# The v stage of a hybrid decoder layer: tile norms, transposes and sums placed ahead of the former tile's products, norm_g broadcast by a matmul, four store buffers

## The chip, the cores and the metric

The kernel runs on one core of a Trainium2 chip. A core has five engines that each work through a queue of their own in order: TensorE (PE) multiplies matrices and transposes, VectorE (DVE) and GpSimd (POOL) do elementwise work, ScalarE (ACT) does functions, copies and casts, and SyncE (SP) issues most of the DMA transfers. They meet only through semaphores. The metric is the device time of one execution in microseconds (us); lower is better.

## The reference

The layer norms its input `x` (1024 tokens by 1024 channels), projects it with one wide matrix `w_in`, runs a gated short convolution and a dilated attention beside each other, merges both by two gates, projects again and adds the residue. Cut to what matters here:

```
def rms_norm(x, g):
    xf = x.astype(jnp.float32)
    y = xf * lax.rsqrt(jnp.mean(xf * xf, axis=-1, keepdims=True) + EPS)
    return (y * g.astype(jnp.float32)).astype(x.dtype)
...
    u = rms_norm(h, norm_g[layer])
...
    proj = jnp.einsum("bsd,dc->bsc", h, w_in)
    xc, bg, cg, zc, q, k, v, za, g_conv, g_attn = jnp.split(proj, splits, axis=-1)
```

The v stage computes the columns `v` of `proj`, a product of 1024x1024 by 1024x1024, and on the way leaves the normed, transposed input in on-chip memory for all later stages.

## The kernel before

Every matrix product is done exactly in float32 by splitting both operands into a high and a low part (float32r) and adding three products: high by high, high by low, low by high. `split` (L77) makes the parts: ACT casts the source to the high part, then DVE, or POOL where it is named, subtracts to get the low part.

The v stage (L125 to L283) is the first of the kernel. The tokens come in eight tiles of 128. `normed(t)` takes one: ACT squares and sums it, `rstd_of` makes the scale in four small DVE operations and one ACT square root, DVE scales the two halves by the scale and by `gb` (norm_g times -0.5, on all 128 partitions), and PE transposes each half by four 128x128 transposes into banks 6 and 7 of PSUM. `into` splits a transposed half into the tables `b11`, `b21` (tiles 0 to 3) and `b22` (tiles 4 to 7).

The product uses seven block products in place of eight, after Strassen and Winograd. The sums of the input blocks, `t1` to `t4`, are made by `sums(j)` from tile 4+j and the tables of tile j: six DVE operations of 128x512 (L194 to L202), each result split again, with the low half on POOL. The sums of weight blocks are made on DVE from `piece`s of 512 KB (two of eight row blocks, all columns of one half), and split by `operand`. `prod` issues six PE products (two row blocks, three each) of 128x512, so one tile of one block product is two calls, 12 products. `added` and `emit` add what was kept aside, split the result and store it to `v_dram`.

The order is: for each of the tiles 0 to 3 in turn, `normed`, `into`, its b11 products, its b21 products, `added` (L231 to L241). Then the weight sums, `sums(0)` to `sums(3)`, and the block products t1, t2, b22, t3 and t4, each for all four tiles, by halves of the weight rows (`product`, L250). A scheduler reorders instructions within each engine's queue by its own times and by when buffers come free; so what stands in the code is not quite what stands in a queue. Buffers that matter: three slots for x tiles (`xt`), four for raw weights (`raw`), four for split weights (`v_hi`, `v_lo`), two for split results before their store (`v2`), eight PSUM banks.

After the v stage, `sec` (L293) computes all other column blocks in the same way, with weights in place of tokens as the split operand (`a_hi`, `a_lo`).

Of the kernel before, what the change touches and what calls it, by code (L numbers as in the profile page):

```python
# [11 lines left out]
F32 = mybir.dt.float32  # L12
F32R = mybir.dt.float32r
AF = mybir.ActivationFunctionType
OP = mybir.AluOpType
# [3 lines left out]
P = 128  # L19
S = 1024  # L20
D = 1024
# [2 lines left out]
LAST = (4, 6, 0, 2)  # L24
ACTP = 5
ACTL = 3
WARM = 22
HD = 64
NP = NH // 2
NB = S // P  # L30
# [10 lines left out]
def layer(ctx, tc, x, norm_g, w_blk, w_v, b_merge, conv_w, w_conv, w_attn, w_o, final_g, tab, sel_in, selb_in, out):  # L41
    nc = tc.nc
    ctx.enter_context(nc.allow_low_precision("float32 operands are split exactly into float32r pairs"))

    const = ctx.enter_context(tc.tile_pool(name="const", bufs=1, reuse_waits="tile"))
# [3 lines left out]
    ps = ctx.enter_context(tc.tile_pool(name="ps", bufs=1, space=PSUM))  # L49
# [22 lines left out]
    def bank(first=0, n=8):  # L72

        i = turn[first, n] = (turn.get((first, n), -1) + 1) % n
        return ps.tile([P, 512], F32, tag=f"bank{first + i}", name="bank")
# [42 lines left out]
    H = NK // 2  # L118
# [6 lines left out]
    with tc.tile_pool(name="p0", bufs=2, reuse_waits="tile") as p0:  # L125
        gb = p0.tile([P, D], F32, name="gb", bufs=1)
        xt = {}

        def load_x(i):
            xt[i] = p0.tile([P, D], F32, name="xt", bufs=3)  # L130
            nc.sync.dma_start(xt[i], x[i * P:(i + 1) * P, :])

        def piece(c, d, kh):

            raw = wr.tile([P, 2, 512], F32, tag="raw", name="raw")
            k = 4 * d + 2 * kh
            nc.sync.dma_start(raw, w_v[c, :, k:k + 2, :])
            return raw

        def operand(raw, eng=None):  # L140
            hi = p0.tile([P, 2, 512], F32R, name="v_hi", bufs=4)
            lo = p0.tile([P, 2, 512], F32R, name="v_lo", bufs=4)
            split(hi, lo, raw, eng)
            return hi, lo


        warm = bank(6, 2)
        for _ in range(WARM):
            nc.tensor.transpose(warm[:, :P], ident, ident)
        load_x(0)  # L150
        nc.sync.dma_start(gb, norm_g.to_broadcast([P, D]))
        nc.vector.tensor_scalar(gb, gb, -0.5, None, op0=OP.mult)
        raws = [piece(0, 0, 0), piece(0, 0, 1)]
        load_x(1)
        raws += [piece(0, 1, 0), piece(0, 1, 1)]
        load_x(2)
        a1 = [operand(r, nc.gpsimd if i else nc.vector) for i, r in enumerate(raws)]

        def normed(t):

            if t + 3 < NB:
                load_x(t + 3)
            sq = p0.tile([P, D], mybir.dt.bfloat16, tag="vc", name="sq")
            ss = small.tile([P, 1], F32, name="ss")
            nc.scalar.activation(sq, xt[t], AF.Square, accum_out=ss)
            rs = small.tile([P, 1], F32, name="rs")
            rstd_of(ss, rs)
            xs = xt[t]
            for g in range(2):
                gs = slice(g * 512, g * 512 + 512)  # L170
                nc.vector.scalar_tensor_tensor(xs[:, gs], xt[t][:, gs], rs, gb[:, gs], op0=OP.mult, op1=OP.mult)
                pt = bank(6, 2).rearrange("p (k q) -> p k q", k=4)
                for k in range(4):
                    nc.tensor.transpose(pt[:, k, :], xs[:, (4 * g + k) * P:(4 * g + k + 1) * P], ident)
                yield pt

        def into(n, j, src, eng=None):
            tt = slice(j * P, (j + 1) * P)
            split(ub[n][0][:, :, tt], ub[n][1][:, :, tt], src, eng)

        def of(n, j):
            return [f(y[:, :, j * P:(j + 1) * P]) for y in ub[n]]

        def sums(j):

            c12 = p0.tile([P, H, P], F32, name="c12", bufs=1)
            c22 = p0.tile([P, H, P], F32, name="c22", bufs=1)
            for n, pt in enumerate(normed(H + j)):
                nc.scalar.copy(c22 if n else c12, pt)
                if n:  # L190
                    into("b22", j, pt)
            t1, t2, t4 = (p0.tile([P, H, P], F32, name="ts", bufs=3) for _ in range(3))
            b11, b21 = of("b11", j), of("b21", j)
            nc.vector.tensor_sub(t1, c12, b11[0])  # L194
            nc.vector.tensor_sub(t1, t1, b11[1])
            into("t1", j, t1, nc.gpsimd)
            nc.vector.tensor_sub(t2, c22, t1)
            into("t2", j, t2, nc.gpsimd)
            nc.vector.tensor_sub(c12, c22, c12)
            into("t3", j, c12, nc.gpsimd)  # L200
            nc.vector.tensor_sub(t4, b21[0], t2)
            nc.vector.tensor_add(t4, t4, b21[1])  # L202
            into("t4", j, t4, nc.gpsimd)

        def prod(pt, n, j, kh, op, first=False):

            tt = slice(j * P, (j + 1) * P)
            bhi, blo = ub[n]
            hi, lo = op
            for i in range(2):  # L210
                k = 2 * kh + i
                more = dict(skip_group_check=not first)
                nc.tensor.matmul(pt, bhi[:, k, tt], hi[:, i, :], start=first and k == 0, stop=False, **more)  # L213
                nc.tensor.matmul(pt, bhi[:, k, tt], lo[:, i, :], start=False, stop=False, **more)  # L214
                nc.tensor.matmul(pt, blo[:, k, tt], hi[:, i, :], start=False, stop=k == H - 1, **more)

        def emit(c, t, v):
            v2 = p0.tile([P, 8, 2, HD], F32R, name="v2")
            split(v2[:, :, 0, :], v2[:, :, 1, :], v.rearrange("p (h d) -> p h d", h=8))
            nc.sync.dma_start(  # L220
                v_dram[4 * c:4 * c + 4, :, t * 256:(t + 1) * 256].rearrange("n p e -> p n e"),
                f(v2).rearrange("p (n a) s d -> p n (a s d)", n=4))

        def added(c, t, pt, v):
            vc = p0.tile([P, 512], F32, name="vc")
            nc.vector.tensor_add(vc, pt, v)
            emit(c, t, vc)

        chain = [ps.tile([P, 512], F32, tag=f"bank{j}", name="bank") for j in range(H)]
        x1 = []  # L230
        for j in range(H):  # L231
            for n, pt in zip(("b11", "b21"), normed(j)):
                into(n, j, pt)
            for kh in range(2):
                prod(chain[j], "b11", j, kh, a1[kh], first=True)
            x1.append(p0.tile([P, 512], F32, name="keep1", bufs=4))
            nc.scalar.copy(x1[j], chain[j])
            pt = bank(4, 2)
            for kh in range(2):
                prod(pt, "b21", j, kh, a1[2 + kh], first=True)  # L240
            added(0, j, pt, x1[j])  # L241
        sum_ = []
        for kh in range(2):
            r1, r2 = piece(1, 0, kh), piece(1, 1, kh)
            nc.vector.tensor_add(r1, r1, r2)
            sum_.append(r1)
        for j in range(H):
            sums(j)

        def product(n, pts, ops, first=False):  # L250
            for kh in range(2):
                for j in range(H):
                    prod(pts[j], n, j, kh, ops[kh], first)

        side = [ps.tile([P, 512], F32, tag=f"bank{4 + j}", name="bank") for j in range(H)]
        product("t1", side, [operand(r) for r in sum_], first=True)
        x5 = []
        for j in range(H):
            x5.append(p0.tile([P, 512], F32, name="keep1", bufs=4))
            nc.scalar.copy(x5[j], side[j])  # L260
        for kh in range(2):
            nc.vector.tensor_sub(sum_[kh], sum_[kh], piece(0, 0, kh))
        product("t2", chain, [operand(r) for r in sum_])
        u2 = []
        for j in range(H):
            u2.append(p0.tile([P, 512], F32, name="keep2", bufs=4))
            nc.scalar.copy(u2[j], chain[j])
        for kh in range(2):
            nc.vector.tensor_sub(sum_[kh], piece(0, 1, kh), sum_[kh])
        product("b22", side, [operand(r) for r in sum_])  # L270
        for j in range(H):
            added(0, H + j, side[j], u2[j])
        ops = []
        for kh in range(2):
            r1, r2 = piece(0, 0, kh), piece(1, 0, kh)
            nc.vector.tensor_sub(r1, r1, r2)
            ops.append(operand(r1))
        product("t3", chain, ops)
        for j in range(H):
            added(1, H + j, chain[j], x5[j])  # L280
        product("t4", chain, [operand(piece(1, 1, kh)) for kh in range(2)])
        for j in range(H):
            emit(1, j, chain[j])  # L283
# [497 lines left out]
```

## Time and profile before

| | us |
|---|---|
| median of 3 runs | 1374.81 |
| lowest, highest | 1372.64, 1378.58 |
| the profiled execution | 1380.34 |
| its span | 1378.5 |

| engine | busy us | share of span | instructions |
|---|---|---|---|
| PE | 1304.9 | 95% | 6228 |
| DVE | 843.0 | 61% | 1576 |
| ACT | 645.8 | 47% | 1265 |
| POOL | 257.8 | 19% | 187 |

The page has the whole span in 40 slices of about 34 us, one digit each for the tenths that an engine is busy. PE has 6, 5, 7 and 9 in the first four, and 8 or 9 from then to the last but one. The v stage lies in the first four and a half. The row of the granted clock has 8, 8, 7 and 9 tenths there and 9 or more after it. The chain of work that ended last is 85% PE over the whole span, 6% DMA, 3% each DVE, ACT and time without a cause in the profile ("issue").

A row of a timeline is start, duration, engine, line, operation, written tile, read tiles, shape and count; in brackets stands how long the engine was idle ahead of it and what released it. A PE row's duration contains the fill and drain of the array, so products follow one another in less than it: their pace is read from start to start.

### The profile page before, as it was taken

Reading aid. Unit: us, or ns where it says so; the run is one execution under the profiler, and the core shown is the slowest. Engines: PE = TensorE matmul, PEld = TensorE weight load, DVE = VectorE, ACT = ScalarE, POOL = GpSimd, SP = SyncE. Lnnn points to the kernel's source line nnn. Section 1 sums busy time; section 2 is a strip of 40 time slices with the busy share of each in tenths; the row PEclk is TensorE's granted clock in tenths of the full one; section 3 lists DMA queues with packets and bytes.
Section 4 is the critical chain, followed back from the end, with each engine's and each line's share of the span. In section 5 each row is a group of like instructions: output and inputs, shape, how many; then the busy total and the mean of one; then the engine's idle time right before and its main releaser. Section 6 shows DMA issues by size and latency. Waiting matters only on the chain.

```text
span 1378.5 us, 17657 instructions
## 1 busy us (share of the span) xinstructions
PE 1304.9 (95%) x6228; PEld 1080.1 (78%) x6228; DVE 843.0 (61%) x1576; ACT 645.8 (47%) x1265; POOL 257.8 (19%) x187
## 2 busy tenths in 40 slices
PE   6579899999999999999999998889999999999997
PEld 5358688888888888887888886778888888788886
DVE  3596566655767677676655443657667667554325
ACT  3444344444443434343444455767677768322211
POOL 2051000000010101011000000543444446254000
PEclk8879999999999999999999999999999999999999
DMA  7315444541222313136233324994566475655302
GB/s 259 120 49 198 155 167 168 171 165 62 77 92 62 123 62 107 49 113 197 101 110 112 115 84 114 312 261 135 152 169 161 134 194 188 219 168 186 150 31 92
DMA packets 87072, 192.38 MB, mean 140 GB/s; under 512 B 8456, under 2 KB 33292, under 8 KB 86856
## 3 DMA queue, kind: packets, MB, share of 16 engines
q1 hardware_dynamic: 84184, 182.32, 42.1%
q0 software_dynamic: 2800, 8.94, 1.9%
q8 instruction: 49, 0.80, 0.2%
q14 instruction: 39, 0.32, 0.1%
HBM read 132.91 MB, written 58.31 MB: 139 GB/s over the span
## 4 chain that ended last, share of the span: by engine, by line
PE 85%; DMA 6%; issue 3%; ACT 3%; DVE 3%; POOL 0%; SPq 0%; DVEq 0%; ACTq 0%
PE bank L314 16%; PE bank L315 16%; PE bank L316 16%; PE bank L96 4%; PE bank L98 4%; PE bank L97 4%; PE bank L548 3%; PE bank L559 2%; PE bank L560 2%; PE bank L719 2%; PE bank L717 2%; PE bank L718 2%; PE bank L213 2%; DMA kl<-qk_dram 2%; PE bank L214 2%
## 5 line engine op out<-in xcount | busy, mean ns | idle before, releaser
L314 PE MATMUL bank<-t_hi,a_hi 128*128 128x512 f32 x576 | 225.2, 391 | 2.7 <-DVE sec_o L325 2.3
L315 PE MATMUL bank<-t_lo,a_hi 128*128 128x512 f32 x576 | 224.8, 390 | 0.0
L316 PE MATMUL bank<-t_hi,a_lo 128*128 128x512 f32 x576 | 224.8, 390 | 0.0
L78 ACT CAST a_hi<-s 128x512 fp32r<-128x512 f32 x144 | 89.6, 622 | 191.4 <-PE bank L315 175.2
L314 PE MATMUL bank<-b_hi,a_hi 128*128 128x512 f32 x432 | 169.5, 392 | 4.7 <-ACT a_hi L78 4.7
L315 PE MATMUL bank<-b_lo,a_hi 128*128 128x512 f32 x432 | 168.8, 391 | 0.0
L316 PE MATMUL bank<-b_hi,a_lo 128*128 128x512 f32 x432 | 168.5, 390 | 0.0
L79 DVE TENSOR_TENSOR a_lo<-s,a_hi 128x512 fp32r<-128x512 f32 x144 | 102.1, 709 | 100.1 <-ACT a_hi L78 100.0
L78 ACT CAST a_hi<-raw 128x512 fp32r<-128x512 f32 x108 | 67.1, 621 | 149.3 <-PE bank L315 126.0
L314 PEld LDWEIGHTS bank<-t_hi,a_hi 128*128 128x128 f32 x576 | 108.5, 188 | 25.9 <-DVE sec_o L325 3.0
L315 PEld LDWEIGHTS bank<-t_lo,a_hi 128*128 128x128 f32 x576 | 108.6, 189 | 22.6
L316 PEld LDWEIGHTS bank<-t_hi,a_lo 128*128 128x128 f32 x576 | 108.4, 188 | 22.6
L440 ACT ACTIVATE pr<-pr,nm 128x640 f32<-128x640 f32 (+7 forms) x128 | 99.9, 782 | 24.7 <-DVE nm L435 24.3
L435 DVE CUSTOM_DVE_ANT_0 pr<-bank,bias 128x512 f32<-128x512 f32 (+3 forms) x128 | 72.1, 569 | 48.0 <-PE bank L431 44.5
L314 PEld LDWEIGHTS bank<-b_hi,a_hi 128*128 128x128 f32 x432 | 81.6, 189 | 22.9 <-ACT a_hi L78 6.1
L79 DVE TENSOR_TENSOR a_lo<-raw,a_hi 128x512 fp32r<-128x512 f32 x108 | 74.3, 688 | 39.3 <-ACT a_hi L78 38.3
L316 PEld LDWEIGHTS bank<-b_hi,a_lo 128*128 128x128 f32 x432 | 81.5, 189 | 17.0
L315 PEld LDWEIGHTS bank<-b_lo,a_hi 128*128 128x128 f32 x432 | 81.6, 189 | 16.8
L548 PE MATMUL bank<-ident,pr 128*128 128x128 f32 x576 | 87.5, 275 | 4.4 <-ACT pr L440 4.0
L79 DVE TENSOR_TENSOR pp<-bank,pp 128x512 fp32r<-128x512 f32 x96 | 64.9, 687 | 27.6 <-ACT pp L78 27.1
L430 PE MATMUL bank<-kh,q 128*128 128x256 f32 (+2 forms) x192 | 73.0, 382 | 5.8 <-DVE nm L435 2.1
L548 PEld LDWEIGHTS bank<-ident,pr 128*128 128x128 f32 x576 | 67.9, 141 | 12.3 <-ACT pr L440 6.5
(228 smaller groups left out, 2687.0 us busy)
## 6 DMA issues: line engine op xcount, KB each, us to landing
raw<-in_w_blk SPq DMA_DIRECT2D x72, 512.0 KB, 3.6
raw<-in_w_v SPq DMA_DIRECT2D x18, 512.0 KB, 4.2
v_dram<-v SPq DMA_DIRECT2D x16, 512.0 KB, 3.0
qk_dram<-qk_hi SPq DMA_DIRECT2D x32, 256.0 KB, 2.0
qk_dram<-qk_lo SPq DMA_DIRECT2D x32, 256.0 KB, 2.0
q<-qk_dram SPq DMA_DIRECT2D x32, 256.0 KB, 5.9
kh<-qk_dram SPq DMA_DIRECT2D x32, 256.0 KB, 7.3
kl<-qk_dram SPq DMA_DIRECT2D x32, 256.0 KB, 6.4
```

The costliest lines, as they stand in the source:

```text
L78: nc.scalar.copy(hi, src)
L79: (eng or nc.vector).tensor_sub(lo, src, f(hi))
L96: nc.tensor.matmul(pt, whi[:, k, :], mhi[:, t], start=(k == 0), stop=False)
L97: nc.tensor.matmul(pt, whi[:, k, :], mlo[:, t], start=False, stop=False)
L98: nc.tensor.matmul(pt, wlo[:, k, :], mhi[:, t], start=False, stop=(k == NK - 1))
L314: nc.tensor.matmul(pt, hi[:, k], mhi[:, k], start=first and k == 0, stop=False, **more)
L315: nc.tensor.matmul(pt, hi[:, k], mlo[:, k], start=False, stop=False, **more)
L316: nc.tensor.matmul(pt, lo[:, k], mhi[:, k], start=False, stop=k == H - 1, **more)
L430: nc.tensor.matmul(sc[:, :n], qs, kh[hd][:, c0:c0 + n], start=True, stop=False)
L435: nc.vector.tensor_tensor_reduce(pr[:, c0:c0 + m], sc[:, :m], bias[hd][:, off:off + m], 1.0, 3.0e38 if nm is None else nm, OP.add, OP.min, ...
L440: nc.scalar.activation(pr[:, :nk], pr[:, :nk], AF.Exp, bias=nm, scale=-1.0, accum_out=den[p][:, a, b:b + 1])
L548: nc.tensor.transpose(pt[:, j, i * P:(i + 1) * P], rows[b][:, (kb + j) * P:(kb + j + 1) * P], ident)
```

## The change

Five things are changed, all of them in the v stage.

1. `norm_g` is loaded as one row of 4 KB, from ACT's queue, and spread over the partitions by two matmuls with a column of -0.5 and two ACT copies out of PSUM. Before, a 512 KB broadcast load on SP's queue and a DVE multiplication did it.
2. `normed` and `into` of a tile (`first`) stand before the products of the tile ahead of it (`early`), and `sums(0)` before the last tile's products; the other `sums` stand among the weight sums and the t1 and t2 products.
3. The low halves of `t1` to `t4` are made by DVE in place of POOL. Of the first four weight pieces, three low halves stay on POOL.
4. `product` goes tile by tile, with both halves of the weight rows of a tile behind one another, and t1 and t2 of a tile stand together.
5. Four buffers in place of two for split results (`v2`); `sq` gets a buffer of its own, `keep2` shares the slots of `xt`. The 22 transposes at the start that only keep PE busy become 6, 8 and 12 in three places.

```diff
-WARM = 22
+WARM = 6
+WARM2 = 8
+WARM3 = 12
...
+        nc.scalar.dma_start(gb[0:1], norm_g)
+        ones = const.tile([1, P], F32, name="ones")
+        nc.vector.memset(ones, -0.5)
...
-        nc.sync.dma_start(gb, norm_g.to_broadcast([P, D]))
-        nc.vector.tensor_scalar(gb, gb, -0.5, None, op0=OP.mult)
...
-        a1 = [operand(r, nc.gpsimd if i else nc.vector) for i, r in enumerate(raws)]
+        warm(WARM)
+        for h in range(2):
+            pt = bank(6, 2)
+            nc.tensor.matmul(pt, ones, gb[0:1, h * 512:h * 512 + 512], start=True, stop=True)
+            nc.scalar.copy(gb[:, h * 512:h * 512 + 512], pt)
+        warm(WARM2)
...
-            into("t1", j, t1, nc.gpsimd)
+            into("t1", j, t1)
...
-            v2 = p0.tile([P, 8, 2, HD], F32R, name="v2")
+            v2 = p0.tile([P, 8, 2, HD], F32R, name="v2", bufs=4)
...
+        first(0)
+        warm(WARM3)
+        a1 += [operand(raws[0]), operand(raws[1], nc.gpsimd)]
+        first(1)
+        a1 += [operand(raws[2], nc.gpsimd), operand(raws[3], nc.gpsimd)]
+        early(0)
+        first(2)
+        early(1)
+        first(3)
+        early(2)
+        sums(0)
+        early(3)
...
+        s1 = [operand(r) for r in sum_]
+        sums(1)
...
+        s2 = [operand(r) for r in sum_]
+        sums(2)
...
+        for j in range(H):
+            side.append(ps.tile([P, 512], F32, tag=f"bank{4 + j}", name="bank"))
+            for kh in range(2):
+                prod(side[j], "t1", j, kh, s1[kh], first=True)
+            x5.append(p0.tile([P, 512], F32, name="keep1", bufs=4))
+            nc.scalar.copy(x5[j], side[j])
+            for kh in range(2):
+                prod(chain[j], "t2", j, kh, s2[kh])
...
+            if j == 0:
+                sums(3)
```

On ACT, at the very start of the program, this is the queue before, from the first tile's square to the last split of the first four weight pieces (`v_hi`); `b11_hi` and `b21_hi` are the high halves of the first transposed tile:

```order
L165 ACTIVATE sq_171,ss_172<-xt_133 128x1024
L105 ACTIVATE rs_r_177<-rs_a_175 128x1
L78 CAST v_hi_149<-raw_137 128x1024
L78 CAST v_hi_153<-raw_139 128x1024
L78 CAST b11_hi_92<-bank_185 128x4x128
L78 CAST b21_hi_94<-bank_193 128x4x128
L78 CAST v_hi_157<-raw_143 128x1024
L78 CAST v_hi_161<-raw_145 128x1024
```

And this is the same stretch of ACT's queue now:

```order
L176 ACTIVATE sq_155,ss_156<-xt_113 128x1024
L107 ACTIVATE rs_r_161<-rs_a_159 128x1
L80 CAST v_hi_197<-raw_115 128x1024
L80 CAST v_hi_201<-raw_117 128x1024
L167 COPY gb_109<-bank_134 128x512
L176 ACTIVATE sq_207,ss_208<-xt_119 128x1024
L167 COPY gb_109<-bank_137 128x512
L107 ACTIVATE rs_r_213<-rs_a_211 128x1
L80 CAST v_hi_236<-raw_121 128x1024
L80 CAST v_hi_240<-raw_123 128x1024
L80 CAST b11_hi_92<-bank_169 128x4x128
```

The copies of `gb` stand behind the splits of the first two weight pieces, and the first tile's high halves behind all four.

On PE, between the products of tile 0 and of tile 1, this stood before (`xt_141` is tile 1, `bank_214` takes tile 0's b21 products and `bank_166` tile 1's b11 products):

```order
L213 MATMUL bank_214<-v_hi_161,b21_hi_94 128x512
L214 MATMUL bank_214<-v_lo_162,b21_hi_94 128x512
L215 MATMUL bank_214<-v_hi_161,b21_lo_95 128x512
L174 MATMUL bank_249<-ident_69,xt_141 128x128 x4
L174 MATMUL bank_257<-ident_69,xt_141 128x128 x4
L213 MATMUL bank_166<-v_hi_149,b11_hi_92 128x512
L214 MATMUL bank_166<-v_lo_150,b11_hi_92 128x512
```

And this stands in PE's queue now between tile 1's b11 products (`bank_150`) and its b21 products (`bank_322`); `xt_125` is tile 2:

```order
L225 MATMUL bank_150<-v_lo_202,b11_hi_92 128x512
L226 MATMUL bank_150<-v_hi_201,b11_lo_93 128x512
L185 MATMUL bank_293<-ident_69,xt_125 128x128 x4
L224 MATMUL bank_322<-v_hi_236,b21_hi_94 128x512
L225 MATMUL bank_322<-v_lo_237,b21_hi_94 128x512
L185 MATMUL bank_301<-ident_69,xt_125 128x128 x4
L226 MATMUL bank_322<-v_hi_236,b21_lo_95 128x512
L224 MATMUL bank_322<-v_hi_236,b21_hi_94 128x512
```

The transposes of a tile have moved from the border between two tiles into the products of the tile ahead.

On DVE, in the middle of the stage, this was the queue while one tile's sums were made (`c12`, `c22` are the transposed halves, `ts` the sums):

```order
L194 TENSOR_TENSOR ts_468<-c12_435,b11_hi_92 128x512
L79 TENSOR_TENSOR b22_lo_97<-bank_460,b22_hi_96 128x4x128
L195 TENSOR_TENSOR ts_468<-ts_468,b11_lo_93 128x512
L199 TENSOR_TENSOR c12_435<-c22_436,c12_435 128x512
L103 TENSOR_SCALAR rs_a_587<-ss_584 128x1
L197 TENSOR_TENSOR ts_469<-c22_436,ts_468 128x512
L201 TENSOR_TENSOR ts_470<-b21_hi_94,ts_469 128x512
L107 RECIPROCAL rs_y_591<-rs_r_589 128x1
L202 TENSOR_TENSOR ts_470<-ts_470,b21_lo_95 128x512
```

And this is DVE's queue over the sums of the third of the four tiles now:

```order
L205 TENSOR_TENSOR ts_599<-c12_568,b11_hi_92 128x512
L206 TENSOR_TENSOR ts_599<-ts_599,b11_lo_93 128x512
L210 TENSOR_TENSOR c12_568<-c22_569,c12_568 128x512
L81 TENSOR_TENSOR t4_lo_105<-ts_539,t4_hi_104 128x4x128
L208 TENSOR_TENSOR ts_600<-c22_569,ts_599 128x512
L81 TENSOR_TENSOR t1_lo_99<-ts_599,t1_hi_98 128x4x128
L81 TENSOR_TENSOR t3_lo_103<-c12_568,t3_hi_102 128x4x128
L212 TENSOR_TENSOR ts_601<-b21_hi_94,ts_600 128x512
L81 TENSOR_TENSOR t2_lo_101<-ts_600,t2_hi_100 128x4x128
L213 TENSOR_TENSOR ts_601<-ts_601,b21_lo_95 128x512
```

The four low halves (`t1_lo` to `t4_lo`) of a tile stand among its sums.

## Rows read from the trace of the kernel before

**Rows 1.** Stretches of the v stage: busy us and instructions per engine, granted clock, DMA
```profile
core 0: us, PE busy (x) PEld busy (x) DVE busy (x) ACT busy (x) POOL busy (x), PEclk, DMA share, GB/s
...
26.20:35.80 9.60, 9.54 (x32) 7.37 (x32) 1.91 (x3) 2.80 (x5) 0.00 (x0) 0.69 0.44 162
35.80:39.40 3.60, 0.02 (x1) 0.05 (x1) 2.82 (x8) 0.72 (x2) 0.00 (x0) 0.95 0.14 50
...
60.00:70.50 10.50, 0.05 (x1) 0.08 (x2) 9.08 (x22) 5.12 (x12) 0.00 (x0) 0.64 0.65 207
70.50:100.00 29.50, 21.39 (x82) 15.06 (x82) 27.65 (x34) 15.31 (x30) 16.59 (x11) 0.78 0.16 51
...
104.00:145.80 41.80, 41.80 (x180) 33.63 (x180) 24.26 (x28) 15.83 (x23) 6.20 (x5) 1.00 0.60 200
145.80:153.80 8.00, 3.59 (x9) 2.05 (x8) 4.66 (x8) 2.83 (x5) 0.00 (x0) 0.66 0.58 202
```
**Rows 2.** The chain of waits, two products: start us, us, what
```profile
30.00 0.43 PE bank L214
...
108.20 0.24 PE bank L215
```
**Rows 3.** Timeline of PE at the marks of the stage
```profile
2.98 4.95 PE L149 MATMUL bank<-ident 128*128 128x128 f32 x22 [2.98 <-POOL ident masks.py:199]
...
12.37 0.79 PE L213 MATMUL bank<-v_hi,b_hi 128*128 128x512 f32 x1 [1.99 <-ACT b_hi L78]
...
39.38 1.94 PE L174 MATMUL bank<-ident,xt 128*128 128x128 f32 x8 [3.65 <-issue]
...
84.03 1.04 PE L174 MATMUL bank<-ident,xt 128*128 128x128 f32 x8
...
112.48 1.09 PE L213 MATMUL bank<-v_hi,b_hi 128*128 128x512 f32 x4
...
145.84 0.40 PE L215 MATMUL bank<-v_hi,t_lo 128*128 128x512 f32 x1
...
153.74 0.63 PE L316 MATMUL bank<-b_hi,a_lo 128*128 128x512 f32 x1
```
**Rows 4.** Timeline of ACT at the start and at the end of the stage
```profile
9.37 1.04 ACT L78 CAST v_hi<-raw 128x1024 fp32r<-128x1024 f32 x1 [3.32 <-DMA raw<-in_w_v]
10.66 1.04 ACT L78 CAST v_hi<-raw 128x1024 fp32r<-128x1024 f32 x1 [0.24 <-DMA raw<-in_w_v]
...
18.37 1.06 ACT L165 ACTIVATE sq<-xt 128x1024 bf16<-128x1024 f32 x1
...
146.46 0.58 ACT L78 CAST v<-bank 128x512 fp32r<-128x512 f32 x1 [2.40 <-DMA v_dram<-v]
...
151.19 0.62 ACT L78 CAST a_hi<-raw 128x512 fp32r<-128x512 f32 x1 [1.88 <-DMA v_dram<-v]
```
**Rows 5.** Timeline of POOL: a weight piece's low half and a sum's
```profile
11.79 2.37 POOL L79 TENSOR_TENSOR v_lo<-raw,v_hi 128x1024 fp32r<-128x1024 f32 x1 [8.86 <-ACT v_hi L78]
...
79.42 1.74 POOL L79 TENSOR_TENSOR t_lo<-c,t_hi 128x512 fp32r<-128x512 f32 x1
```
**Rows 6.** Timeline of DVE: a weight sum, then sums beside POOL and without it
```profile
61.74 1.22 DVE L262 TENSOR_TENSOR raw<-raw 128x1024 f32<-128x1024 f32 x1
...
79.94 0.15 DVE L107 RECIPROCAL rs_y<-rs_r 128x1 f32<-128x1 f32 x1
80.05 1.65 DVE L202 TENSOR_TENSOR ts<-ts,b_lo 128x512 f32<-128x512 f32 x1
81.63 1.24 DVE L109 SCALAR_TENSOR_TENSOR rs_t<-rs_y,rs_a 128x1 f32<-128x1 f32 x1
...
85.24 0.68 DVE L194 TENSOR_TENSOR ts<-c,b_hi 128x512 f32<-128x512 f32 x1
85.95 0.69 DVE L195 TENSOR_TENSOR ts<-ts,b_lo 128x512 f32<-128x512 f32 x1
86.56 0.68 DVE L199 TENSOR_TENSOR c<-c,c 128x512 f32<-128x512 f32 x1
```
**Rows 7.** DMA issues of the stage: KB each, median us from issue to landing
```profile
xt<-in_x SPq DMA_DIRECT2D x8, 512.0 KB, 8.1
```

More of the change, by code (lines that the diff above doesn't have):

```diff
@@ L144, in operand, with warm @@
             return hi, lo
-        warm = bank(6, 2)
-        for _ in range(WARM):
-            nc.tensor.transpose(warm[:, :P], ident, ident)
+        nc.scalar.dma_start(gb[0:1], norm_g)
+        ones = const.tile([1, P], F32, name="ones")
+        nc.vector.memset(ones, -0.5)
+        def warm(n):
+            pt = bank(5, 1)
+            for _ in range(n):
+                nc.tensor.transpose(pt[:, :P], ident, ident)
         load_x(0)
-        nc.sync.dma_start(gb, norm_g.to_broadcast([P, D]))
-        nc.vector.tensor_scalar(gb, gb, -0.5, None, op0=OP.mult)
         raws = [piece(0, 0, 0), piece(0, 0, 1)]
@@ L162, in normed @@
                 load_x(t + 3)
-            sq = p0.tile([P, D], mybir.dt.bfloat16, tag="vc", name="sq")
+            sq = p0.tile([P, D], mybir.dt.bfloat16, name="sq", bufs=1)
             ss = small.tile([P, 1], F32, name="ss")
@@ L195, in sums @@
             nc.vector.tensor_sub(t1, t1, b11[1])
-            into("t1", j, t1, nc.gpsimd)
+            into("t1", j, t1)
             nc.vector.tensor_sub(t2, c22, t1)
-            into("t2", j, t2, nc.gpsimd)
+            into("t2", j, t2)
             nc.vector.tensor_sub(c12, c22, c12)
-            into("t3", j, c12, nc.gpsimd)
+            into("t3", j, c12)
             nc.vector.tensor_sub(t4, b21[0], t2)
             nc.vector.tensor_add(t4, t4, b21[1])
-            into("t4", j, t4, nc.gpsimd)
+            into("t4", j, t4)
         def prod(pt, n, j, kh, op, first=False):
@@ L229, in layer, with first, early @@
         chain = [ps.tile([P, 512], F32, tag=f"bank{j}", name="bank") for j in range(H)]
-        x1 = []
-        for j in range(H):
+        x1, a1 = [], []
+        def first(j):
             for n, pt in zip(("b11", "b21"), normed(j)):
                 into(n, j, pt)
+        def early(j):
             for kh in range(2):
@@ L246, in layer, with product @@
             sum_.append(r1)
+        s1 = [operand(r) for r in sum_]
+        sums(1)
+        for kh in range(2):
+            nc.vector.tensor_sub(sum_[kh], sum_[kh], piece(0, 0, kh))
+        s2 = [operand(r) for r in sum_]
+        sums(2)
+        def product(n, pts, ops, first=False):
+            for j in range(H):
+                for kh in range(2):
+                    prod(pts[j], n, j, kh, ops[kh], first)
+        side, x5, u2 = [], [], []
         for j in range(H):
-            sums(j)
-        def product(n, pts, ops, first=False):
+            side.append(ps.tile([P, 512], F32, tag=f"bank{4 + j}", name="bank"))
             for kh in range(2):
[L252 to L258, printed above, removed]
+                prod(side[j], "t1", j, kh, s1[kh], first=True)
             x5.append(p0.tile([P, 512], F32, name="keep1", bufs=4))
             nc.scalar.copy(x5[j], side[j])
[L261 to L266, printed above, removed]
+            for kh in range(2):
+                prod(chain[j], "t2", j, kh, s2[kh])
+            if j % 2 == 0:
+                two = p0.tile([P, 2, 512], F32, tag="xt", name="keep2", bufs=3)
+            u2.append(two[:, j % 2])
             nc.scalar.copy(u2[j], chain[j])
+            if j == 0:
+                sums(3)
         for kh in range(2):
```

## The prediction

> **What bounds the kernel now.** I read the table of the v stage by stretches first [rows 1], because the page's share of busy time is a mean over stages that have different limits. TensorE (PE) does nothing in 35.8 to 39.4 us, behind the second tile's products (gaps of the same kind stand behind the first and the third), nor in 60.0 to 70.5, and it is busy with 82 instructions in half of 70.5 to 100. From 104 it is full until the last product, and then 3.6 of 8 us are work. VectorE (DVE) is the opposite: 9.08 of 10.5 us and 27.65 of 29.5 where PE waits. So the v stage waits on norm, transpose and split, never on products, until 104. Second, the chain of waits [rows 2] gives what one 128x512 product costs: 0.43 us at the granted clock of 1.2 GHz, 0.24 at 2.4. PE falls to the lower level behind each gap (0.64 granted mean in 60.0 to 70.5, 1.00 from 104). Third, PE's own rows [rows 3] give the marks that I shall move: first product at 12.37, end of the four early tiles at 60.0, first b22 product at 112.48, last product at 145.84, and 153.74, the first product with the low half of the next stage's weights. From that mark on the program keeps its 5,807 PE instructions, in the same order for some 3,000 of them; the later differences are swaps of neighbours in the attention stage, which I count at nothing with 3 us either way. Whatever the mark gains, the kernel gains.
>
> **Start.** The change takes a 512 KB load of gb out of SP's queue. The weight pieces land one load apart (ACT splits them at 9.37 and 10.66 [rows 4]), so each comes about 1.3 us sooner and the second high half ends near 10.4 instead of 11.7. But gb is now copied out of PSUM by ACT behind both of these (the order in the section on the change), so the first tile, scaled at 8.2 before, cannot be scaled until 11.0; the second half's copy stands behind the next tile's square (1.06 [rows 4]) and its accumulator read, so about 12.8. The two matmuls that make gb have no row of their kind; they have from about 4.3 (six transposes at 0.225 after 2.98 [rows 3]) until 10.4, so they cost nothing up to 3 us each, and what they cost beyond that comes on top.
>
> GpSimd (POOL) makes the low half of the second piece at that time, 2.37 us [rows 5]. On DVE, the sums that read two SBUF tensors last 1.65 instead of 0.68 beside POOL, a 128x1 one 1.24, and each ends about 0.6 us after a POOL operation does (80.05 plus 1.65 is 81.70, POOL's row ends at 81.16) [rows 5, 6]. The Trainium skill ("SBUF — State Buffer", Who interferes with whom) says that such an instruction and a GpSimd one that reads SBUF exclude each other for a whole instruction, whoever is first. The rows agree, and it speaks against the new order, which puts the scaling of two tiles beside the three POOL splits that stay; with shared bandwidth in its place my sum would gain some 3 us.
>
> By the rows, the first tile's halves are scaled at 12.8 and 13.5. PE then has four transposes (1.94 us for eight at the low clock), twelve warming ones (0.225 each) and four more: 13.6 + 1.0 + 2.7 + 1.0 = 18.3 for the first product, 5.9 later than now.
>
> **The four early tiles.** The transposes of a tile now stand inside the products of the tile before, so the gaps between the tiles go. What is left is PE: 96 products at 0.233 (as 33.4 us for the last 144 give, below; 22.4), 32 transposes at 0.13 (1.04 for eight [rows 3]: 4.2), ten products still at the low clock (10 x 0.2 = 2.0), and 1.0 for low halves held up by POOL: 18.3 + 29.6 = 47.9, against 60.0. DVE has 1.91 + 2.82 us of work per tile and ACT 2.80 + 0.72 [rows 1], PE 24 products and 8 transposes (6.6 at the high clock), so they keep pace.
>
> **The sums and the t1, t2 products.** Here DVE is the bound. From about 23 us, when the second tile's low half is done, until b22's operands, its queue holds 16 operations of 1,024 columns (1.2 each [rows 6]: 19.2), 69 of 512 columns, the 16 low halves that POOL did among them (0.61 where nothing depends, 0.71 where the next needs the last [rows 6], so 0.65: 44.9) and six chains of four small ones (0.15 to 0.2: 4.2): 68.3. The 16 cost 10.4; without POOL beside it, DVE gets back 0.97 on each of the eight long sums (7.8) and 1.0 on a small one, so the move alone is worth nothing much, and the gain comes from where the work stands: beside the products of the early tiles instead of behind them. Without waits it ends at 91.3, and b22's operands stand some four operations (4 us) before the end, at 87.3. Waits on ACT's high halves are what I can only bound: nothing, or all 16 exposed with 0.62 plus a hand-over of 0.1 (11.5), and as much as 4 more for the copies. Most have other work beside them in the order, so I take 3.2: b22 starts at 90.5, against 112.48. The products t1 and t2 of a tile (24 at 0.24, 5.8 us, or 10.3 at the low clock) fit beside a tile's work on DVE (six sums, two scalings, five low halves, one chain: 9.2 us) at the high clock and nearly at the low one.
>
> **The rest and the tail.** b22, t3 and t4 are 144 products, 33.4 us from 112.48 to 145.84, and PE is already full there: unchanged, the last one starts at 123.9. The new product order (both halves of a tile, then the next tile) finishes a bank every 2.8 us, and the four store buffers let ACT split it at once: now the cast at 146.46 waited 2.40 for a store, and the next stage's split at 151.19 another 1.88 [rows 4]. After the last product come one cast (0.58), its low half (0.69), two sums of the next stage (1.3) and a low half (0.7): the low-half product starts 3.5 after the last, at 127.4. It was 7.9, so 4.4 of the gain is the tail's. The second low half of that stage may still wait for the last store, but 10 products are queued ahead of it.
>
> 153.7 - 127.4 = 26.3. The profiled execution took 1380.34 (span 1378.5 and 1.84 around it); it is 5.5 above the median of the runs, 1374.81. So 1354 by its own time, **1349** against the median.
>
> **Rivals.** (a) PE-bound: DVE has no waits, POOL disturbs little and the clock rises early. Then b22 starts near 84 and the mark gains 33 to 37: 1340. For it: DVE is never more than 1 to 2 us idle in 60 to 100. Against: each low half in DVE's queue has an ACT operation ahead of it, and no hand-over is free. (b) DVE waits: each low half on DVE now stands in one queue with everything else and waits for ACT, which waits for DVE. With the upper bound of 15.5 instead of 3.2 the mark gains 14, 1361. For it: the low halves were on POOL, where only the products waited for them. (c) The v stage moves but the gain is lost to loads and low clock: under 7 us, 1371. (d) The other side: tiles land late. SP issues in order, and the loads of the last two x tiles now stand behind stores of the first products, which wait for DVE. A tile load took 8.1 us from issue to landing in the middle [rows 7]; were four of them met in full, with ACT's square and everything behind it on ACT and DVE stopped, that would be 32 us, 6 more than the gain: 1381. It decides from 6.5 us of lateness a tile; against it, a tile's slot now comes free earlier, since its transposes stand earlier.
>
> **Chances.** My forecast (gain 18 to 32, 1343 to 1357) 0.58; (a) 0.12; (b) and what lies between it and (c) 0.19; (c) 0.06; (d) 0.05. Half a per cent, 6.9 us, is about what a measurement of this kernel can tell from no change. Faster by more than that: 0.89, same 0.06, slower 0.05. The range leaves out the far ends of (a) and of (b), and (c), (d): 1337 to 1363.
>
> **What would show it.** In the profile after: the first product near 18; no gap above 1.5 us on PE between 20 and 46; long sums back to 0.7 us on DVE and DVE over nine tenths busy from 25 to 88 while PE idles in it; b22 near 90, and the same 33.4 us behind it; under 4 us from the last v product to the first low-half product. A first product past 21, a tile waiting on its load, or DVE idle for more than 10 us before b22 would make it wrong.

## The result and the profile after

The changed kernel takes 1352.61 us (median of 4 runs, 1352.28 to 1354.75); the kernel before took 1375.02 beside it (1372.64 to 1378.58). The ratio is 0.984, 95% interval 0.981 to 0.986: 22.4 us less. 1349 was predicted, 1337 to 1363 as range. The profiled execution has a span of 1353.0 us against 1378.5.

The first view of the changed kernel is the table by stretches that answers to [rows 1]; the stretches are cut at its own marks. Columns as there: each engine's busy time with its instructions, then the granted clock as a share of 2.4 GHz, the DMA share and GB/s.

```profile
18.90:46.40 27.50, 27.50 (x130) 22.33 (x130) 19.90 (x43) 13.11 (x27) 0.00 (x0) 0.94 0.59 185
46.40:64.10 17.70, 9.42 (x30) 6.46 (x28) 17.66 (x28) 10.68 (x20) 0.00 (x0) 0.80 0.49 154
64.10:90.00 25.90, 22.07 (x85) 16.83 (x86) 23.93 (x39) 14.94 (x26) 0.00 (x0) 0.81 0.13 41
90.00:124.20 34.20, 34.20 (x148) 27.41 (x146) 19.64 (x25) 10.96 (x16) 0.10 (x1) 1.00 0.77 263
124.20:127.80 3.60, 2.21 (x9) 0.99 (x7) 2.64 (x5) 2.25 (x4) 0.00 (x0) 1.00 0.66 230
```

TensorE (PE) is full from 18.9 to 46.4, where the kernel before had its gaps between the tiles. Then VectorE (DVE) is the bound: it is busy for 17.66 of 17.7 and 23.93 of 25.9 us. GpSimd (POOL) does nothing in these two stretches any more. From 79.9 PE is full again (its row below), until its last product of the stage, and 3.6 us lie behind that.

PE's rows, which answer to [rows 3]; the brackets hold the idle time before a row and what ended it:

```profile
15.48 0.71 PE L224 MATMUL bank<-v_hi,b_hi 128*128 128x512 f32 x1
16.03 0.40 PE L225 MATMUL bank<-v_lo,b_hi 128*128 128x512 f32 x1
18.90 0.67 PE L185 MATMUL bank<-ident,xt 128*128 128x128 f32 x4 [2.46 <-DVE rs_a L105]
...
45.70 0.39 PE L226 MATMUL bank<-v_hi,b_lo 128*128 128x512 f32 x1
...
49.09 0.50 PE L224 MATMUL bank<-v_hi,t_hi 128*128 128x512 f32 x1 [2.56 <-ACT t_hi L80]
...
79.91 0.49 PE L226 MATMUL bank<-v_hi,t_lo 128*128 128x512 f32 x1 [1.03 <-DVE t_lo L81]
...
90.75 1.09 PE L224 MATMUL bank<-v_hi,b_hi 128*128 128x512 f32 x4
...
124.11 0.40 PE L226 MATMUL bank<-v_hi,t_lo 128*128 128x512 f32 x1
125.70 0.50 PE L348 MATMUL bank<-b_hi,a_hi 128*128 128x512 f32 x1 [1.19 <-ACT a_hi L80]
...
127.72 0.49 PE L350 MATMUL bank<-b_hi,a_lo 128*128 128x512 f32 x1
```

The mark that the prediction moved, the first low-half product of the next stage, comes at 127.72; it was at 153.74. That is 26.0 us, where the spans differ by 25.5; behind the mark the profile shows 1225.3 us against 1224.8.

DVE's scalings at the start, and what POOL does beside them (answering to [rows 5, 6]):

```profile
8.91 2.34 DVE L182 SCALAR_TENSOR_TENSOR xt<-xt,rs,gb 128x512 f32<-128x512 f32 x1 [0.68 <-ACT gb L167]
11.24 0.74 DVE L182 SCALAR_TENSOR_TENSOR xt<-xt,rs,gb 128x512 f32<-128x512 f32 x1
12.59 5.66 DVE L182 SCALAR_TENSOR_TENSOR xt<-xt,rs,gb 128x512 f32<-128x512 f32 x2
18.16 0.68 DVE L81 TENSOR_TENSOR b_lo<-bank,b_hi 128x512 fp32r<-128x512 f32 x1
18.77 0.14 DVE L105 TENSOR_SCALAR rs_a<-ss 128x1 f32<-128x1 f32 x1
```

```profile
8.35 2.35 POOL L81 TENSOR_TENSOR v_lo<-raw,v_hi 128x1024 fp32r<-128x1024 f32 x1 [5.42 <-ACT v_hi L80]
12.56 5.13 POOL L81 TENSOR_TENSOR v_lo<-raw,v_hi 128x1024 fp32r<-128x1024 f32 x2 [1.86 <-ACT v_hi L80]
```

A scaling of 0.7 us takes 2.34 and 2.8 beside POOL. The pair of 5.66 ends at 18.25, 0.6 after POOL's row does. Behind it in DVE's queue stand the first tile's first low half and then the small operation that PE's row at 18.90 names in its bracket; that is why PE starts for good at 18.9 only.

### The profile page after: what moved, and what is told of

Its sections match the earlier page's. It is cut to its first block, busy times and chain, and to the rows that moved or that the text cites. A ratio compares the mean times of both kernels' runs of the same rounds, so it can differ in the third digit from the quotient of the medians.

```text
span 1353.0 us, 17649 instructions
## 1 busy us (share of the span) xinstructions
PE 1301.0 (96%) x6236; PEld 1076.5 (80%) x6236; DVE 845.1 (62%) x1592; ACT 644.7 (48%) x1267; POOL 233.9 (17%) x171
## 4 chain that ended last, share of the span: by engine, by line
PE 84%; DMA 7%; DVE 4%; ACT 3%; issue 1%; POOL 0%; DVEq 0%; ACTq 0%; POOLq 0%; SPq 0%
PE bank L348 17%; PE bank L349 17%; PE bank L350 17%; PE bank L98 4%; PE bank L100 4%; PE bank L99 4%; PE bank L582 3%; PE bank L593 2%; PE bank L594 2%; PE bank L753 2%; PE bank L752 2%; PE bank L751 2%; DMA vp<-v_dram 2%; DMA m_dram<-sg 2%; PE bank L226 2%; PE bank L464 2%
## 5 line engine op out<-in xcount | busy, mean ns | idle before, releaser
L349 PEld LDWEIGHTS bank<-t_lo,a_hi 128*128 128x128 f32 x576 | 108.4, 188 | 22.4
L474 ACT ACTIVATE pr<-pr,nm 128x640 f32<-128x640 f32 (+7 forms) x128 | 99.8, 782 | 25.5 <-DVE nm L469 25.2
L350 PEld LDWEIGHTS bank<-b_hi,a_lo 128*128 128x128 f32 x432 | 81.1, 188 | 17.2 <-DVE a_lo L81 0.3
```

Of the source, the lines that this page charges most:

```text
L349: nc.tensor.matmul(pt, hi[:, k], mlo[:, k], start=False, stop=False, **more)
L350: nc.tensor.matmul(pt, lo[:, k], mhi[:, k], start=False, stop=k == H - 1, **more)
L474: nc.scalar.activation(pr[:, :nk], pr[:, :nk], AF.Exp, bias=nm, scale=-1.0, accum_out=den[p][:, a, b:b + 1])
```

## The experiments

Twelve kernels were run. The whole times of one kernel spread by 2 to 13 us from run to run, so the table has the ratio to the kernel before with its interval beside marks of one profile: first product, first b22 product, last v product, and "low", the first low-half product behind the v stage. "Behind" is the span less "low".

| kernel | ratio (95%) | first | b22 | last v | low | behind |
|---|---|---|---|---|---|---|
| before | 1 | 12.37 | 112.48 | 145.84 | 153.74 | 1224.8 |
| changed | 0.984 (0.981 to 0.986) | 15.48 | 90.75 | 124.11 | 127.72 | 1225.3 |
| e1, t halves on POOL | 0.987 (0.982 to 0.991) | 16.96 | 99.36 | 132.73 | 136.35 | 1228.2 |
| e2, two stores | 0.985 (0.981 to 0.988) | 15.40 | 90.76 | 124.12 | 129.95 | 1219.8 |
| e3, tiles in turn | 0.984 (0.981 to 0.987) | 15.11 | 88.25 | 121.62 | 125.23 | 1229.6 |
| e4, no POOL | 0.974 (0.971 to 0.977) | 13.39 | 84.62 | 117.99 | 121.60 | 1218.4 |
| e5, sq shared | 0.984 (0.980 to 0.988) | 15.44 | 90.54 | 123.91 | 127.50 | 1227.5 |
| e6, in turn and sq shared | 0.996 (0.994 to 0.998) | 17.93 | 107.90 | 141.26 | 144.88 | 1223.9 |
| e7, before, sq its own | 0.985 (0.981 to 0.989) | 12.49 | 94.92 | 128.28 | 134.56 | 1218.9 |
| e8, before, t halves on DVE | 1.001 (0.999 to 1.003) | 12.43 | 106.63 | 140.00 | 147.49 | 1227.6 |
| e9, gb by a load | 0.981 (0.978 to 0.984) | 12.94 | 90.08 | 123.44 | 127.06 | 1220.3 |
| e10, order by halves | 0.982 (0.979 to 0.985) | 15.64 | 90.42 | 123.79 | 127.39 | 1221.6 |
| e11, e4 and four x tiles | 0.974 (0.972 to 0.977) | 14.19 | 80.87 | 114.23 | 117.85 | 1224.8 |
| e12, e11 in turn | 0.976 (0.973 to 0.978) | 14.83 | 82.43 | 115.79 | 119.41 | 1220.9 |

**What makes the overlap: e3, e5, e6, e7.** First the tiles' written order was undone.

```
-        first(1); a1 += [...]; early(0); first(2); early(1)
-        first(3); early(2); sums(0); early(3)
+        a1 += [...]; early(0); first(1); early(1); first(2)
+        early(2); first(3); early(3)      # sums(0) ahead of s1
```

> The changed kernel with the order of the early tiles undone: a tile is normed, transposed and split, then its products run, then the next tile; the sums begin behind the fourth tile's products. Low halves on VectorE, matmul broadcast, four stores and the new block order stay. My theory (the gain is the overlap): TensorE has its gaps of 3 to 4 us behind three tiles again and the first sums stand behind the products, so the marker (127.7) comes 10 to 14 us later, at 138 to 142; ratio 0.991 to 0.994. Rival (gain from the earlier loads at the start, the engine of the low halves and the tail): marker later by under 4 us.

The mark did not come 10 to 14 us later but 2.5 earlier. The theory that the written order carries the gain fell, and so did the picture behind it: the scheduler puts the next tile's transposes among the products by itself. Then why not in the kernel before? There the square's scratch tile `sq` has its slots in common with `vc`, the sum of a tile's products; the change gives it its own buffer. Putting that one word back, alone (e5) and with the tiles in turn (e6), and giving it to the kernel before, alone (e7):

```
-            sq = p0.tile([P, D], mybir.dt.bfloat16, name="sq", bufs=1)
+            sq = p0.tile([P, D], mybir.dt.bfloat16, tag="vc", name="sq")     # e5, e6; e7 the other way
```

> The changed kernel, but the square's scratch tile sq shares the two slots of vc again, as in the kernel before (one word; order of the code as changed). New theory behind e3: what put the tiles' transposes behind the former tile's products was that sq had to wait for a slot of vc, which is given back by the split of that tile's result; the order of the code decides little. Then the transposes of the third and later tiles stand behind products again, 2 or 3 gaps of 3 to 4 us return, and the marker (first low-half product behind the v stage, 127.7) comes 6 to 10 us later, 134 to 138; ratio to the kernel before 0.988 to 0.992. Rival (the written order carries the overlap): marker within 2 us of 127.7.

> The changed kernel with the early tiles written in turn (as in e3) and sq in the slots of vc again: TensorE's order is then that of the kernel before, eight transposes and 24 products four times. Theory (sq's slot): all gaps behind the tiles return, marker (127.7; 125.2 for the tiles in turn alone) at 137 to 142. Rival (the overlap is worth little, and the engine of the low halves is everything): marker under 131.

> The kernel before with one word changed: sq has a buffer of its own. Everything else as before: tiles in turn, gb by a load of 512 KB, low halves of t on GpSimd, two stores, products by half. Theory (sq's slot): the overlap of the early tiles comes back by this word alone; marker (153.7) at 141 to 148, ratio 0.991 to 0.996. Rival (written order, or low halves on GpSimd, hold it all): marker within 2 us of 153.7.

With both undone the mark is at 144.88, 17.2 later (2.5 of it already at the first product) and beyond the 142 that I expected at most; with either alone it stays (127.50, 125.23). The kernel before gains 19.2 at the mark by that one word, more than I expected, and its ratio of 0.985 can't be told from the changed kernel's. So e5's theory (the slot alone decides) was wrong too: each of the two is enough. PE's rows of e6 have the gaps of the kernel before again:

```profile
28.21 1.71 PE L185 MATMUL bank<-ident,xt 128*128 128x128 f32 x8 [4.06 <-issue]
...
40.37 1.94 PE L185 MATMUL bank<-ident,xt 128*128 128x128 f32 x8 [3.64 <-issue]
...
53.43 1.94 PE L185 MATMUL bank<-ident,xt 128*128 128x128 f32 x8 [3.64 <-issue]
...
72.32 2.88 PE L185 MATMUL bank<-ident,xt 128*128 128x128 f32 x12 [10.76 <-issue]
```

"issue" names no engine; the cause is read on ScalarE (ACT) and DVE. e6, ACT and then DVE, behind the first tile's products:

```profile
21.87 0.59 ACT L252 COPY keep<-bank 128x512 f32<-128x512 f32 x1 [5.53 <-PE bank L226]
22.35 1.06 ACT L176 ACTIVATE sq<-xt 128x1024 bf16<-128x1024 f32 x1
```

```profile
24.26 0.69 DVE L237 TENSOR_TENSOR vc<-bank,keep 128x512 f32<-128x512 f32 x1 [6.07 <-PE bank L226]
24.87 0.14 DVE L105 TENSOR_SCALAR rs_a<-ss 128x1 f32<-128x1 f32 x1
```

The next tile's square stands in ACT's queue behind the copy that waits for this tile's products, and its norm on DVE behind their sum. In e7 the square stands ahead of that copy, and the transposes of a tile fall between products in fours:

```profile
12.81 1.07 ACT L165 ACTIVATE sq<-xt 128x1024 bf16<-128x1024 f32 x1
...
18.02 0.59 ACT L237 COPY keep<-bank 128x512 f32<-128x512 f32 x1 [2.07 <-PE bank L215]
```

```profile
28.65 0.60 PE L174 MATMUL bank<-ident,xt 128*128 128x128 f32 x4
...
31.42 0.60 PE L174 MATMUL bank<-ident,xt 128*128 128x128 f32 x4
```

That the scheduler hands out the slots of one name in written order, and so can't take a square past an earlier `vc`, fits all four kernels; the rule itself was not tested apart.

**Which engine makes the low halves: e1, e8, e4.** e1 puts the sixteen low halves of t1 to t4 back on POOL, e8 puts them on DVE in the kernel before, e4 takes the last three splits off POOL.

```
-            into("t1", j, t1)                                 # e1, so for t2, t3, t4; e8 the other way
+            into("t1", j, t1, nc.gpsimd)
```

```
-        a1 += [operand(raws[2], nc.gpsimd), operand(raws[3], nc.gpsimd)]     # e4, and for raws[1]
+        a1 += [operand(raws[2]), operand(raws[3])]
```

> The changed kernel with one thing undone: the sixteen low halves of t1 to t4 are made on GpSimd again. Marker: the first low-half product of the stage behind the v stage, at 127.7 us in the changed kernel. My theory (the gain is where the work stands, and the engine that makes these halves hardly matters): VectorE loses 16 x 0.65 = 10.4 us of work in 46 to 90, and gets about 8 us back as sums that wait for GpSimd (0.68 to 1.65), so the marker stays at 125 to 131 and the ratio to the kernel before at 0.982 to 0.987. Rival 1 (the gain is that VectorE and GpSimd no longer disturb each other): marker past 135, ratio 0.99 or more. Rival 2 (VectorE is the bound and was overloaded by the change): marker near 118, ratio 0.976.

> The kernel before with the sixteen low halves of t1 to t4 on VectorE. By the step of my prediction (10.4 us of work more, 8.8 back from GpSimd's disturbance): marker (153.7) at 152 to 156, ratio 0.998 to 1.002. By what e1 showed (8.6 us lost when they go back to GpSimd): marker at 143 to 147, ratio 0.993 to 0.996.

> The changed kernel with the last three splits on GpSimd (low halves of the weight pieces at the start) moved to VectorE: no GpSimd work beside VectorE in the v stage. My theory (the two exclude each other): the scalings that took 2.34 and 2 x 2.83 us go back to 0.70 each (5.9 us less) against 3 x 1.22 more on VectorE, so the second tile is transposed about 2 to 3 us before 18.9 and the marker (127.7) comes 1 to 3 us earlier; time 0 to 0.3% under the changed kernel. Rival (VectorE bounds the stage by its work): marker 2 to 4 us later. Rival (x tiles land late whatever the start does): marker within 0.7 us, the wait of the square for its tile grows by what the start gained.

e1 put the mark 8.6 later (rival 1 by the mark, 135 or later; the ratio of 0.987 is still the theory's, and its interval overlaps that of the changed kernel). The groups on DVE in its sums, 46 to 100 us (busy time, mean ns of one):

```profile
L182 DVE SCALAR_TENSOR_TENSOR xt<-xt,rs,gb 128x512 f32<-128x512 f32 x4 | 5.8, 1490 | 0.0
L212 DVE TENSOR_TENSOR ts<-b_hi,ts 128x512 f32<-128x512 f32 x4 | 5.4, 1354 | 0.2
L213 DVE TENSOR_TENSOR ts<-ts,b_lo 128x512 f32<-128x512 f32 x4 | 4.7, 1164 | 0.1
L208 DVE TENSOR_TENSOR ts<-c,ts 128x512 f32<-128x512 f32 x4 | 3.8, 950 | 0.0
```

and the same in the changed kernel, with one of the sixteen's groups:

```profile
L81 DVE TENSOR_TENSOR t_lo<-ts,t_hi 128x512 fp32r<-128x512 f32 x12 | 8.2, 684 | 0.0
L182 DVE SCALAR_TENSOR_TENSOR xt<-xt,rs,gb 128x512 f32<-128x512 f32 x4 | 2.8, 746 | 0.0
L208 DVE TENSOR_TENSOR ts<-c,ts 128x512 f32<-128x512 f32 x4 | 2.7, 684 | 0.0
L212 DVE TENSOR_TENSOR ts<-b_hi,ts 128x512 f32<-128x512 f32 x4 | 2.7, 684 | 0.0
L213 DVE TENSOR_TENSOR ts<-ts,b_lo 128x512 f32<-128x512 f32 x4 | 2.7, 683 | 0.0
```

Sixteen halves at 0.684 are 10.9 us. Against that, the four groups of e1 lose 3.0 + 2.7 + 1.9 + 1.1, and two sums and the weights' halves, which are not shown, another 3: 11.7. DVE's work comes out even, as predicted, though the second term was larger (I had 8.8). In the kernel before the move is worth nothing in time (e8), but 6.3 at the mark. Together with the 19.2 of the scratch tile's own buffer (e7) that is 25.4 of the change's 26.0 at the mark; the kernel before with just these two edits was not run, so it is not shown how little the rest of the change adds. What e1 adds is a later start (3.0 at the first t1 product) and waits: DVE is busy for 46.44 us of 46.4 to 99.4, idle 6.6, against 2.0 in 46.4 to 90 of the changed kernel.

e4 gains more than any theory said: 6.1 at the mark, and a ratio whose interval lies wholly under the changed kernel's. DVE's rows of e4 at the start:

```profile
7.09 2.49 DVE L81 TENSOR_TENSOR v_lo<-raw,v_hi 128x1024 fp32r<-128x1024 f32 x2 [0.27 <-ACT v_hi L80]
9.50 0.74 DVE L182 SCALAR_TENSOR_TENSOR xt<-xt,rs,gb 128x512 f32<-128x512 f32 x1
10.49 0.75 DVE L182 SCALAR_TENSOR_TENSOR xt<-xt,rs,gb 128x512 f32<-128x512 f32 x1 [0.18 <-ACT gb L167]
11.44 1.23 DVE L81 TENSOR_TENSOR v_lo<-raw,v_hi 128x1024 fp32r<-128x1024 f32 x1 [0.19 <-ACT v_hi L80]
...
14.83 1.41 DVE L182 SCALAR_TENSOR_TENSOR xt<-xt,rs,gb 128x512 f32<-128x512 f32 x2
```

Four low halves on DVE cost 1.23 each, and the second tile's scalings end at 16.2 instead of 18.25, those of the third at 19.9 instead of 23.8. The last product of the early tiles starts at 39.82 instead of 45.70, so nearly all of the 6.1 is made there. The rest of e4's gain, 6.9 us behind the mark, is not explained: that part lies between 1218.4 and 1229.6 in these kernels. It is not made next to the v stage: the first 2,000 PE instructions behind the mark take 453.4 to 454.8 us in all fourteen traces, and the kernels part only later. Nor does the order of PE's queue settle it: the changed kernel, e2 and e12 have the same order there and 1225.3, 1219.8 and 1220.9, and e1, with e4's order, has 1228.2.

**The tail: e2, e10.**

```
-            v2 = p0.tile([P, 8, 2, HD], F32R, name="v2", bufs=4)          # e2
+            v2 = p0.tile([P, 8, 2, HD], F32R, name="v2")
```

```
-            for j in range(H):                                             # e10
-                for kh in range(2):
+            for kh in range(2):
+                for j in range(H):
                     prod(pts[j], n, j, kh, ops[kh], first)
```

> The changed kernel with two store buffers in place of four. My theory (tail): the last v_hi/v casts wait for a store again, as 2.40 and 1.88 us in the kernel before, so the marker (first low-half product behind the v stage, 127.7) comes 3 to 4.5 us later at 131 to 132 and the last v product stays at 124.1; ratio to the kernel before 0.986 to 0.988. Rival (the new product order, a bank every 2.8 us, makes the tail short by itself): marker later by under 1 us.

> The changed kernel with the products b22, t3 and t4 in the old order (first halves of all four tiles, then second halves); four store buffers stay. In the kernel before, last v product to first low-half product of the next stage took 7.9 us, in the changed kernel 3.6, and with two store buffers alone (e2) 5.8. Theory (the order of the products gives the rest of the tail's gain): last v product within 1 us of 124.1, and 5 to 6.5 us from it to the marker, which comes at 129.5 to 131. Rival (with four buffers the order is worth nothing): 3.6 to 4.2 us, marker under 128.5.

From the last v product to the mark it is 7.9 us before, 3.6 in the changed kernel, 5.8 in e2, 3.6 in e10. So four buffers are enough (three do as well: 3.6 in e11 and e12), and with them the order of the b22, t3 and t4 products is worth nothing. Where there are two, the old order has 6.3 (e7) to 7.9 us against e2's 5.8, so it is worth 0.5 to 2 us there. e2's theory had the mechanism but not the size, e10's theory fell. ACT's rows of e2 have the store's waits again:

```profile
124.78 0.59 ACT L80 CAST v<-bank 128x512 fp32r<-128x512 f32 x1 [2.38 <-DMA v_dram<-v]
126.23 0.59 ACT L80 CAST v<-bank 128x512 fp32r<-128x512 f32 x1 [0.87 <-DMA v_dram<-v]
```

**gb: e9.**

```
-        nc.scalar.dma_start(gb[0:1], norm_g)
+        nc.sync.dma_start(gb, norm_g.to_broadcast([P, D]))     # behind load_x(0)
+        nc.vector.tensor_scalar(gb, gb, -0.5, None, op0=OP.mult)
-            nc.tensor.matmul(pt, ones, gb[0:1, ...], start=True, stop=True); nc.scalar.copy(gb[:, ...], pt)
+            for _ in range(4): nc.tensor.transpose(pt[:, :P], ident, ident)
```

> The changed kernel with gb loaded again as a 512 KB broadcast through SP's queue, behind the first x tile, and scaled by VectorE; ordinary warming transposes stand where the two matmuls were. Theory (the broadcast by matmul costs time at the start: e7 starts at 12.5 and reaches b22 at 94.9 with GpSimd's halves, e1 at 17.0 and 99.4): first product at 12 to 14 (15.5 now), marker (first low-half product behind the v stage, 127.7) at 122 to 125. Rival (VectorE's work in the middle of the stage swallows it): marker within 1.5 us of 127.7. Rival (the weights' earlier landing is worth more than the late gb): marker at 130 or later.

The first product comes 2.5 earlier, the mark 0.7: the first rival. DVE shows why: the second tile's scalings, again beside POOL, end at 20.7, later than in the changed kernel.

```profile
17.47 3.21 DVE L183 SCALAR_TENSOR_TENSOR xt<-xt,rs,gb 128x512 f32<-128x512 f32 x2
```

In time the two can't be told apart, so the broadcast by matmul is not shown to gain anything.

**Versions to beat both: e11, e12.**

```
             xt[i] = p0.tile([P, D], F32, name="xt", bufs=4)      # 3 before; v2 has bufs=3
```

> A version to beat both: e4 (no GpSimd split in the v stage) with four buffers for x tiles in place of three, and three store buffers in place of four to make room. In e4 the squares still wait 0.5 to 3.9 us for their tiles, which can only be loaded when a slot is free. Theory (late tiles): these waits go, marker at 118 to 120.5 (e4: 121.6), ratio to the kernel before 0.971 to 0.974. Rival (VectorE's work bounds, the tiles' waits are covered): marker within 1 us of 121.6.

> A version to beat both: e11 with the early tiles written in turn as in e3 (which brought the marker 2.5 us forward there). Theory (the parts add): marker at 115.5 to 119, ratio to the kernel before 0.969 to 0.973. Rival (e3's gain came from the wait behind GpSimd at the start, which is gone here): marker within 1 us of e11's.

e11's mark comes 3.7 us before e4's, just past the near end of what the theory gave (118 to 120.5), but not by its reason: ACT's squares still wait for tiles. What makes the 3.7 is open.

```profile
29.84 1.06 ACT L176 ACTIVATE sq<-xt 128x1024 bf16<-128x1024 f32 x1 [3.55 <-DMA xt<-in_x]
35.65 1.06 ACT L176 ACTIVATE sq<-xt 128x1024 bf16<-128x1024 f32 x1 [2.60 <-DMA xt<-in_x]
```

In time e11 and e12 (medians 1342.56 and 1342.64) can't be told from e4 (1340.91). The parts don't add: e12's mark is 1.6 later than e11's, outside the ranges of its theory and of its rival, where "in turn" alone had brought 2.5.

## Why the prediction was right

| step | predicted | measured |
|---|---|---|
| first product | 18.3 | 15.48 for two, behind 18.90 for the rest |
| end of the early tiles | 47.9 | 46.1 |
| first b22 | 90.5 | 90.75 |
| b22 to last v product | 33.4 | 33.36 |
| last v product to low half | 3.5 | 3.61 |
| gain at the mark | 26.3 | 26.0 |

**Start.** Two terms were mis-sized, against each other. The weight pieces came 3.4 us sooner, not 1.3 (ACT splits them at 5.95 and 7.22, against 9.37 and 10.66 in [rows 4]), so gb's copies ran at 8.29 and 9.83, not at 10.4 and behind. The matmuls for gb stayed under the 3 us each that I had allowed. On the other side POOL's splits cost more than the 1.0 us that I put down for late low halves: they held the scalings of the second tile, 5.66 us for 1.4. (The 3 us that I named for shared bandwidth are in no term of my sum, which has only this 1.0 for POOL.) The sentence on who excludes whom (the Trainium skill, "SBUF — State Buffer", Who interferes with whom) was borne out here by the rows above and by e4, where these scalings are back at 0.7; I quoted it and priced it too low.

**Early tiles.** That the transposes stand inside the products was right, and worth 17 us (e6). I spoke of the written order, and read it from the new kernel's queues, so the number held; which edit makes it I had not asked. Either the order or the scratch tile's own buffer does, and the latter got no word in my working.

**Middle.** DVE as bound from the early tiles to near b22 was right: 41.59 of 43.6 us busy in 46.4 to 90. PE is without gaps already from about 80, where I had b22 as the border. That b22 came within 0.25 us of the forecast is luck. My sum has DVE as the bound from 23 us on, but until 46.4 PE was full and DVE busy for 16.49 of 23.4:

```profile
23.00:46.40 23.40, 23.40 (x118) 19.01 (x116) 16.49 (x36) 12.32 (x25) 0.00 (x0) 1.00 0.58 176
```

From 23 to 90 it worked for 58.1 us, where the sum has 64.3 up to b22's operands, and was idle for 8.9, where I had put 3.2 for waits. Work priced too high (operations of 512 columns follow one another at 0.60 us, not 0.65) and waits priced too low cancel. "The move alone is worth nothing much" was wrong at the mark, by 6.3 in the kernel before (e8) and 8.6 in the changed one (e1); in time neither shows.

**Tail.** Right in size; I gave the order of the products a part in it that it has not got.

**Rivals.** (b) and (c) didn't come; DVE's waits add up to 2 us in 46.4 to 90. (a) didn't come either, with b22 at 90.75, but e4 comes near its numbers (b22 at 84.62, the mark 32.1 sooner, 1340.91) by one of the conditions that it named, that POOL disturbs little. (d) came in part, below its point of decision: one square waits 4.53 us for its tile, the next 0.57.

```profile
36.73 1.06 ACT L176 ACTIVATE sq<-xt 128x1024 bf16<-128x1024 f32 x1 [4.53 <-DMA xt<-in_x]
...
44.04 1.06 ACT L176 ACTIVATE sq<-xt 128x1024 bf16<-128x1024 f32 x1 [0.57 <-DMA xt<-in_x]
```

PE is full there, but DVE, the bound behind it, stands idle for 2.21 us behind the first of them; what that costs at the mark is not shown.

**Behind the mark** I allowed 3 us either way; these kernels show up to 6.4 below the kernel before's 1224.8 and 4.8 above it. So "whatever the mark gains, the kernel gains" does not hold in general: e8 gains 6.3 at the mark and nothing in time. That the change itself came within 0.5 us there is luck in part. Of the 3.6 us between 1349 and 1352.61 most is this: I took a gain between profiled executions off a median, and the one of before stood 5.5 above its median, the one of the changed kernel 2.1.

## What to carry to other kernels

Where a scheduler fills the queues, ask first which buffers tie two steps together: a scratch tile that shares its slots with a result kept the next tile's work behind this tile's products, and one word on it was worth as much as the whole change in time, and 19.2 of its 26.0 us at the mark. Price a move between VectorE and GpSimd in the stretch where it lands, with every two-input instruction of the other engine in it: e8 and e1 are one edit, worth 6.3 us at the mark in one kernel and 8.6 in the other, where adding up work on DVE alone gave nothing. When several edits serve one purpose, undo them one at a time and all together: singly e3, e5 and e10 showed nothing to lose.

## What the hardware showed beyond what was expected

POOL and DVE took turns, one instruction each. Of the four scalings beside POOL's three splits only the one that fell between two of them took 0.74 us. The pair that took 5.66 met two splits, and each scaling waited for one: the first ran from 12.59 to 15.48, 0.55 past the end of POOL's first split (12.56 and 2.37), the second, below, until 0.55 past the end of the next. Nor was POOL spared: its second split began while the first scaling still ran, and took 2.80 us, not 2.37.

```profile
15.40 2.84 DVE L182 SCALAR_TENSOR_TENSOR xt<-xt,rs,gb 128x512 f32<-128x512 f32 x1
```

```profile
14.89 2.80 POOL L81 TENSOR_TENSOR v_lo<-raw,v_hi 128x1024 fp32r<-128x1024 f32 x1
```

Two float32 matmuls of 1x512 with one row to contract show as four records, 3.78 us in all:

```profile
4.45 3.78 PE L166 MATMUL bank<-gb,ones 1*128 1x512 f32 x4
```
